# RNN gates of a hybrid block: from three passes for each gate over 128 channels to two passes for both gates of 64 channels

## The chip, the cores and the metric

The kernel runs on 1 core of one Trainium2 chip. The metric is the device time of one execution in microseconds; the time before is the median of three runs, 3054.97 us (3051.18 to 3057.45). A run differs from the next by about 0.1 to 0.2%.

## The reference

Two layers of a transformer-like block work on 512 tokens and on 256 context tokens (in the second layer the context gives only keys, values and the start of the recurrence). Each layer projects the normed input to eight kinds of 1024 columns, and runs three branches side by side: a gated linear recurrence (RG-LRU), differential attention with 8 heads, and a depthwise convolution; a gated merge, a projection and a SwiGLU follow. All of it is float32.

The change is in the recurrence. For each direction `d` and each of 16 blocks of 64 channels there are two small weight matrices of 64x64, `rnn_w_a` and `rnn_w_x`:

```python
r = sigmoid(blockdiag(x, w_a, b_a))          # x: (tokens, 16 blocks, 64) @ (16, 64, 64)
i = sigmoid(blockdiag(x, w_x, b_x))
log_a = -8 * r * softplus(-lam)
a, b = exp(log_a), sqrt(-expm1(2 * log_a)) * (i * x)
h[t] = a[t] * h[t-1] + b[t]                  # d = 0 forward, d = 1 backward; ctx first, its end starts x
y_r = ((h_forward + h_backward) * gelu(gate projection)) @ w_rnn_o
```

## The kernel before

Channels lie on partitions, tokens along the free dimension: 512 of x and 256 of the context, 768 columns in all (`TA`), taken as the two ranges 512 and 256 (`SEG`). A block is 128 channels; a layer has 8. Every large product is a `Job` of the `Stream` (L368, `kstep`): float32 operands are split into a high and a low part of the format fp32r, and high x high, high x low and low x high are added up in PSUM, three passes. The split of the weights is a cast on ScalarE (`whi`, L515) and a subtraction on VectorE (`wlo`, L520), that of activations the same (`split_steps`, L923 and L929).

The order of the instructions of TensorE, ScalarE and VectorE is written out ahead by a planner (`Plan`): each `step` has an engine, an estimated time, what it waits for, a `prio` (the lowest goes first among those that are ready) and slots that it takes (`acq`) and gives back (`rel`): 3 PSUM tiles `sq`, 2 `small`, 11 SBUF tiles `t`, 16 `a`. The engines then follow that order; each is in order. TensorE's steps of prio 9 are the stream of products, whose order is fixed by the list of jobs; all other steps of TensorE go ahead of it when they are ready.

In each layer the list of jobs is, after the convolution's: `rx_job` 0 to 2 and `rg_job` 0 and 1 among fill jobs, eight `c_job`, then for b = 2 to 7 `rx_job(b + 1)`, `rg_job(b)` and `FILL_RNN[l][b]` fill jobs, then the first head's `q_job` and `k_job`, then eight `r_job`. An `r_job` is the product with `w_rnn_o`; it goes through the operand `ar` block by block, so that its last eighth waits for the recurrence of block 7 (`ar[7]`, written at L923 and L929). Nothing of the stream can pass it.

A block's recurrence is this chain: `rx_job` gives the projection; ScalarE takes it out of PSUM (L1071, L1072), VectorE does a 4-tap convolution (L1076 to L1087), `high` and `low` split it into `k.xh` and `k.xl` of 128 partitions (L1098 on ScalarE, L1101 on VectorE). `rg_job`'s start loads the gate weights (four DMAs, L1115) into `gw`, four 128x128 matrices (gate a or x, direction 0 or 1), each with two 64x64 blocks on its diagonal and zeros elsewhere, and splits them (L1120, L1121). `rnn_steps` then has for each direction and gate one `gate` on TensorE (L1163: three passes of 512 and 256 columns) and one `bend` on ScalarE (L1168: tanh of 128x768 out of PSUM). The gates of block b wait for `em` of block b - 1, those of a block share `sq` with the stream. Then follow on ScalarE L1179, L1184, L1187, on VectorE L1190 and L1194, on ScalarE two square roots with a table load before and after them (L1198, L1236), on VectorE L1201, the scans (L1209, L1212), the sum and the product with the gelu (L1216, L1220), and the split into `ar`. Priorities: what empties PSUM for the stream 0, the weights' split 0.5, the gates 1, the bends 2, the rest of the recurrence 3, the sums of the modulation on VectorE (L603) 4.

Of the kernel before, what the change touches and what calls it, by code (L numbers as in the profile page):

```python
# [18 lines left out]
P = 128  # L19
D = 1024  # L20
NB = D // P
S = 512
# [8 lines left out]
# columns of the parameter tile  # L31
# [4 lines left out]
# gate and value blocks after each block of the convolution and before each step of its norm; after each RNN block  # L36
FILL = [[3, 3, 3, 3, 3, 3, 3, 3, 0, 3], [0, 2, 2, 2, 3, 3, 3, 3, 4, 1]]
FILL_RNN = [[0, 0, 0, 1, 0, 0, 2, 0, 0], [0, 0, 0, 0, 1, 1, 1, 0, 4]]
# products of the stream before the second head's scores
# [3 lines left out]
# the blocks of 1024 in the modulation  # L43
SH1, SC1, GA1, SH2, SC2, GA2 = range(6)

class Step:
    """a share of an engine: what it waits for, about how long it takes (us), what it emits, which slots it takes
    and gives back"""
# [6 lines left out]
@functools.lru_cache(None)  # L55
def slots(text):
    """"t2 sq" is two slots of t and one of sq"""
    return tuple((w.rstrip("0123456789"), int(w.lstrip("abcdefghijklmnopqrstuvwxyz") or 1)) for w in text.split())


class Plan:
    """orders what the engines do: a step goes out once its engine is free and what it waits for is there, the
    lowest prio first, by estimates of the times. The tensor engine fills its time from a stream of products."""
# [15 lines left out]
    def chain(self, eng, fns, *deps, prio=2.0):  # L79
        """steps one after the other, each (time, what it emits, slots taken, slots given back)"""  # L80
        for time, f, *sl in fns:
            sl += [""] * (2 - len(sl))
            deps = (self.step(eng, time, f, *deps, prio=prio, acq=sl[0], rel=sl[1]),)
        return deps[0]
# [29 lines left out]
    def run(self, head):  # L114
        """until all is out; head() gives the stream's next step"""
# [32 lines left out]
class Blocks(list):  # L148
    """channel blocks of a product's moving operand, with the steps that make them, for ranges of tokens"""
# [6 lines left out]
class Job:  # L156
    """a block of 128 columns of a product, for (tokens from, how many, place in PSUM); its token ranges at a time"""
# [7 lines left out]
# ranges of tokens where a norm comes between products: from, how many, place in PSUM  # L165
# [14 lines left out]
def kernel(ctx: ExitStack, tc: tile.TileContext, x, c, ctxt, c_ctx, w_mod, b_mod, g_norm1, g_norm2,  # L180
# [24 lines left out]
    def ttr():  # L205
        return tt(F32R)
# [27 lines left out]
    sinT = cp.tile([P, S], F32, tag="sinT", name="sinT")  # L234
    gw = cp.tile([P, 4, P], F32, tag="gw", name="gw")
    gp.memset(gw, 0.0)
# [49 lines left out]
    def param_vec(l, r, ps):  # L286
        r.p = cp.tile([P, NP], F32, tag=f"par{l}", name=f"par{l}")
        vec.tensor_copy(r.p, ps[:, 0:NP])
        # halves for the tanh form of the sigmoid (what stands in front of it and behind it),
        # an eighth for the query  # L290
# [6 lines left out]
    def param_ends(l, r):  # L297
        """the rest of a layer's parameters, as steps"""
# [10 lines left out]
        # c2 = -4 softplus(-lambda); softplus(y) = max(y, 0) + 2 atanh(w / (2 + w)), w = exp(-|y|)  # L309
# [24 lines left out]
        # minus lambda of the differential attention  # L334
# [13 lines left out]
    def mod_scale(r, i):  # L348
        """a norm's gain times 1 + scale"""
# [13 lines left out]
    def kstep(ps, x, hi, lo, k, nk, segs):  # L363
        """adds the k-th 128 channels to a block of the product"""
# [14 lines left out]
    def start():  # L379
# [20 lines left out]
        # the first two blocks of the modulation, 128 columns of both at a time; the first weights between them  # L400
# [42 lines left out]
    # adds up rows 0, 64 and 1, 65 and 32, 96 and 33, 97  # L443
# [15 lines left out]
    class Stream:  # L459
        """the products in order, an eighth of a block a step; weights come two blocks ahead"""  # L460
# [5 lines left out]
        def add(self, items):  # L466
            """blocks one after the other; ("abreast", some) go together, as their operand comes slowly;
            ("ranges", some) by ranges of tokens; ("late", some) wait for the operand's last block together"""
# [24 lines left out]
        def prep(self):  # L493
            """the two parts of the next blocks' weights, where there is a place"""
# [83 lines left out]
    def mod_sums(r, l, b0, b1, nb, ahead_n, *after):  # L578
        """a layer's modulation of channel blocks b0 to b1, its products added up on DVE, nb blocks at a time"""
# [36 lines left out]
        def ends(c, s):  # L616
            box = []

            def rows():
                """three blocks of a vector to a group of 32 rows"""  # L620
# [118 lines left out]
    class Total:  # L739
        """coef times the sum over channels of what comes block by block, on all partitions: four blocks at a time  # L740
        in groups of 32 rows; the last user gives sq back"""
# [39 lines left out]
    class Squares:  # L781
        """the mean over channels of the squares of what comes block by block, for ranges of tokens, tokens on
        partitions: the first blocks' are added up on PE (in groups of 32 rows) or on DVE, the last block's come in
        at the end"""
# [6 lines left out]
        def feed(self, j, src, dep, part=None):  # L791
            """block j, whole or one range of it"""
# [46 lines left out]
        def rstd(self, g=0):  # L839
            """1 / sqrt(the mean + EPS) of a range; tokens on partitions"""  # L840
# [5 lines left out]
            def turn(i):  # L846
                """both sums' columns"""
# [984 lines left out]
```

## Time and profile before

| what | value |
|---|---|
| median of 3 runs | 3054.97 us (3051.18 to 3057.45) |
| profiled execution, first to last instruction | 3049.5 us |
| TensorE busy | 2999.3 us, 98% of the span |
| VectorE busy | 2062.7 us, 68% |
| ScalarE busy | 1345.6 us, 44% |
| mean granted clock of TensorE | 0.994 of full speed |

The page gives the profiled execution's time as its span; the runs' median lies 5.5 us above it, which takes in what is around the first and the last instruction. The share of a busy engine is an average over stages: VectorE and ScalarE are nearly full in some (the recurrence, about 440 to 720 us and 2050 to 2310 us) and half idle in others.

### The profile page before, as it was taken

How to read it: one execution, taken by the hardware profiler on the slowest of the kernel's cores; microseconds unless marked ns; L12 is line 12 of the kernel's file. 1: busy time of each engine (PE TensorE's matmuls, PEld its weight loads, DVE VectorE, ACT ScalarE, POOL GpSimd, SP SyncE). 2: the span in 40 equal slices, each digit the busy share in tenths (PEclk: the TensorE clock that was granted, in tenths of full speed). 3: DMA queues.
4: the chain of work that ended last, by engine and by line, in shares of the span. 5: the costliest groups of instructions: out<-in, count | busy, mean ns of one | idle time of the engine just before them, and what ended most of it. 6: DMA issues, size and time to landing. Idle time of an engine off the chain costs nothing.

```text
span 3049.5 us, 42300 instructions
## 1 busy us (share of the span) xinstructions
PE 2999.3 (98%) x16809; PEld 2535.6 (83%) x16809; DVE 2062.7 (68%) x2934; ACT 1345.6 (44%) x2153; POOL 120.9 (4%) x292
## 2 busy tenths in 40 slices
PE   8999999999999999999999999999999999999999
PEld 6888888888888788888888897888887887888887
DVE  5998887998577754888222269988785777543334
ACT  5222255685377633321111252347784666342223
POOL 0000000000001101000000000000001010000000
PEclk9999999999999999999999999999999999999999
DMA  8322224435321233555222233334235323433332
GB/s 254 98 89 92 85 83 149 154 95 181 106 63 53 80 113 117 170 198 178 63 63 63 63 104 107 119 105 133 80 99 165 89 63 94 139 90 97 97 97 83
DMA packets 451055, 333.34 MB, mean 109 GB/s; under 512 B 24033, under 2 KB 405882, under 8 KB 450857
## 3 DMA queue, kind: packets, MB, share of 16 engines
q1 hardware_dynamic: 442025, 294.71, 31.9%
q0 software_dynamic: 8832, 35.92, 3.3%
q8 instruction: 132, 2.16, 0.3%
q14 instruction: 66, 0.54, 0.1%
HBM read 281.29 MB, written 40.89 MB: 106 GB/s over the span
## 4 chain that ended last, share of the span: by engine, by line
PE 92%; ACT 3%; DVE 2%; SPq 1%; issue 1%; DMA 1%; ACTq 0%; DVEq 0%
PE sq L368 81%; PE sq L1442 4%; PE small L1477 3%; PE small L1468 2%; PE sq L1163 1%; SPq L407 1%; ACT t L1453 1%; PE small L1318 0%; DMA raw<-in_w_ffn_in_dram 0%; PE small L623 0%; DVE wlo L520 0%; PE small L1545 0%; PE small L853 0%; ACT whi L515 0%; ACT t L1168 0%
## 5 line engine op out<-in xcount | busy, mean ns | idle before, releaser
L368 PE MATMUL sq<-u,whi 128*128 128x512 f32 (+1 forms) x6624 | 1597.0, 352 | 7.6 <-ACT t L1301 1.6
L368 PEld LDWEIGHTS sq<-u,whi 128*128 128x128 f32 x6624 | 1069.8, 189 | 185.3 <-issue 8.8
L368 PE MATMUL sq<-u,wlo 128*128 128x512 f32 (+1 forms) x3312 | 968.8, 351 | 1.0 <-DVE wlo L520 1.0
L515 ACT CAST whi<-raw 128x1024 fp32r<-128x1024 f32 (+1 forms) x348 | 360.3, 1036 | 628.9 <-PE sq L368 585.4
L368 PEld LDWEIGHTS sq<-u,wlo 128*128 128x128 f32 x3312 | 540.9, 189 | 85.7 <-DVE wlo L520 1.5
L520 DVE TENSOR_TENSOR wlo<-raw,whi 128x1024 fp32r<-128x1024 f32 (+1 forms) x348 | 420.6, 1209 | 255.5 <-ACT whi L515 252.0
L368 PE MATMUL sq<-a,whi 128*128 128x512 f32 (+1 forms) x2160 | 531.3, 354 | 0.9 <-ACT t L1453 0.5
L995 DVE SCALAR_TENSOR_TENSOR t<-t,par 128x783 f32<-128x783 f32 (+1 forms) x464 | 399.2, 891 | 8.2
L368 PEld LDWEIGHTS sq<-a,whi 128*128 128x128 f32 x2160 | 352.5, 189 | 60.8 <-issue 2.3
L368 PE MATMUL sq<-a,wlo 128*128 128x512 f32 (+1 forms) x1080 | 326.6, 354 | 0.0
L368 PEld LDWEIGHTS sq<-a,wlo 128*128 128x128 f32 x1080 | 179.3, 188 | 28.1
L1575 DVE SCALAR_TENSOR_TENSOR t<-sq,mod,t 128x512 f32<-128x512 f32 (+1 forms) x102 | 62.2, 633 | 200.2 <-PE sq L368 193.7
L603 DVE SCALAR_TENSOR_TENSOR t<-t,sT 128x512 f32<-128x512 f32 (+1 forms) x224 | 185.6, 881 | 7.8 <-DMA t<-in_w_mod_dram 7.7
L1453 ACT ACTIVATE t<-sq,s 128x768 f32<-128x768 f32 (+1 forms) x160 | 130.2, 820 | 42.9 <-DVE s L1446 39.7
L1446 DVE TENSOR_REDUCE s<-sq 128x1 f32<-128x768 f32 (+1 forms) x160 | 128.9, 845 | 29.0 <-PE sq L1442 28.8
L1442 PE MATMUL sq<-t 128*128 128x512 f32 (+3 forms) x576 | 132.1, 402 | 1.3 <-ACT t L1453 1.3
L1634 DVE TENSOR_TENSOR t<-sq,t 128x768 f32<-128x768 f32 (+1 forms) x44 | 36.3, 825 | 141.9 <-PE sq L368 128.9
L1623 ACT ACTIVATE t<-sq 128x768 f32<-128x768 f32 (+1 forms) x44 | 31.0, 705 | 220.3 <-PE sq L368 214.3
L1442 PEld LDWEIGHTS sq<-t 128*128 128x128 f32 (+1 forms) x576 | 72.4, 187 | 54.7 <-issue 38.4
L1301 ACT ACTIVATE t<-sq,par 128x768 f32<-128x768 f32 (+1 forms) x48 | 38.2, 796 | 134.0 <-PE sq L368 133.9
L1257 DVE SCALAR_TENSOR_TENSOR t<-t,sq 128x768 f32<-128x768 f32 (+1 forms) x48 | 39.2, 819 | 75.0 <-PE sq L368 73.2
L1366 ACT CAST t<-t 64x768 fp32r<-64x768 f32 (+3 forms) x96 | 73.2, 762 | 23.0 <-DVE t L1361 16.5
(235 smaller groups left out, 2697.6 us busy)
## 6 DMA issues: line engine op xcount, KB each, us to landing
raw<-in_w_in_dram SPq DMA_DIRECT2D x160, 512.0 KB, 3.8
raw<-in_w_ffn_in_dram SPq DMA_DIRECT2D x88, 512.0 KB, 3.8
t<-in_w_mod_dram SPq DMA_DIRECT2D x64, 384.0 KB, 4.9
t<-in_w_mod_dram SPq DMA_DIRECT2D x64, 256.0 KB, 4.0
raw<-in_w_ffn_out_dram SPq DMA_DIRECT2D x32, 512.0 KB, 3.9
thg<-t POOLq DMA_DIRECT2D x24, 384.0 KB, 2.6
t<-thg SPq DMA_DIRECT2D x24, 384.0 KB, 4.4
raw<-in_w_conv_o_dram SPq DMA_DIRECT2D x16, 512.0 KB, 4.1
```

Source lines behind the costliest of these rows:

```text
L368: pe.matmul(ps[:, at_:at_ + n], a[k], b[:, s0:s0 + n], start=(k == 0 and i == 0), stop=(k == nk - 1 and i == 2))
L515: act.copy(t[:, 0:w], rt[:, q * n:q * n + w])
L520: vec.tensor_sub(o[:, 0:w], rt[:, q * n:q * n + w], t[:, 0:w].bitcast(F32))
L603: vec.scalar_tensor_tensor(a[:, 0:W], tiles[i][:, 0:W], f, a[:, 0:W], op0=ALU.mult, op1=ALU.add)
L995: vec.scalar_tensor_tensor(acc[:, 0:W], zp[:, k:k + W], r.p[:, i:i + 1], acc[:, 0:W], op0=ALU.mult, op1=ALU.add)
L1366: act.copy(x[i][rows, 0:n], t[src, 0:n])
L1442: pe.matmul(sps[m][:, s0:s0 + n], q[2 if i else m][mr, qsl], k[m][mr, s0:s0 + n], start=(i == 0), stop=(i == 1))
L1446: vec.tensor_reduce(mx[:, m:m + 1], sps[m][:, k0:TA], axis=AX.X, op=ALU.max, negate=True)
L1453: act.activation(es[m][:, 0:kw], sps[m][:, k0:TA], AF.Exp, bias=mx[:, m:m + 1], accum_out=sm[:, m:m + 1])
L1468: pe.transpose(tps[:, i:i + P], es[0][:, g0 + i:g0 + i + P], ident)
L1477: pe.matmul(ops[0][:, 0:P], wt[0][:, i * P:(i + 1) * P], vbox[0][:, vb * P:(vb + 1) * P], start=(i == 0), stop=(i == nk - 1))
L1575: vec.scalar_tensor_tensor(hj[:, ss], ps[:, at_:at_ + n], r.mod[:, ga * 8 + j, v:v + 1], hj[:, ss], op0=ALU.mult, op1=ALU.add)
```

## The change

The stationary operand of a gate product now has the a gate and the x gate of the same 64 channels beside each other (64 + 64 columns), and the same weights on both partition halves; the moving operand has the high part of these 64 channels on one half and the low part on the other. One pass gives the high weights times both parts, a second the low weights times both parts. For each direction there are two such products (`e`, the two halves of the block's channels), each followed by two tanh of 64 partitions. For the second half the columns are x gate, a gate, so the output of a gate may lie on the other half than its channels. The casts and subtractions of the split are by halves, each half's after the other's; the weights are loaded twice, once for each partition half; the memset of `gw` goes. The lines that only drop comments are left out.

```diff
-    gp.memset(gw, 0.0)
...
+        half = slice(0, 64), slice(64, P)
...
-                def high():
-                    k.xh, k.xl = ttr(), ttr()
-                    act.copy(k.xh[:, 0:TA], k.xr[:, 0:TA])
-                def low():
-                    vec.tensor_sub(k.xl[:, 0:TA], k.xr[:, 0:TA], k.xh[:, 0:TA].bitcast(F32))
-                e = step(ACT, act_time(TA), high, k.conv, prio=pr, acq="t2")
-                k.parts = step(DVE, vec_time(TA), low, e, prio=pr)
+                def high(e):
+                    if e == 0:
+                        k.x2 = ttr(), ttr()
+                    act.copy(k.x2[e][half[e], 0:TA], k.xr[half[e], 0:TA])
+                def low(e):
+                    vec.tensor_sub(k.x2[e][half[1 - e], 0:TA], k.xr[half[e], 0:TA],
+                                   k.x2[e][half[e], 0:TA].bitcast(F32))
+                k.parts = []
+                for i in range(2):
+                    e = step(ACT, act_time(TA), lambda i=i: high(i), k.conv, *k.parts[-1:], prio=pr,
+                             acq="" if i else "t2")
+                    k.parts.append(step(DVE, vec_time(TA), lambda i=i: low(i), e, prio=pr))
...
-                    for g, wsrc in ((0, rnn_w_a), (2, rnn_w_x)):
+                    for g, wsrc in ((0, rnn_w_a), (1, rnn_w_x)):
                         for e in range(2):
-                            sy.dma_start(gw[64 * e:64 * e + 64, g:g + 2, 64 * e:64 * e + 64],
-                                         wsrc[l, :, 2 * b + e].rearrange("d i o -> i d o"))
+                            c0 = 64 * (g ^ e)
+                            for hr in half:
+                                sy.dma_start(gw[hr, 2 * e:2 * e + 2, c0:c0 + 64],
+                                             wsrc[l, :, 2 * b + e].rearrange("d i o -> i d o"))
...
-            def gate(box, g):
+            def gates_of(box, d, e):
                 box.append(sq())
-                for s0, n in SEG:
-                    for i, (a, x_) in enumerate(((gwh, k.xh), (gwh, k.xl), (gwl, k.xh))):
-                        pe.matmul(box[0][:, s0:s0 + n], a[:, g, :], x_[:, s0:s0 + n], start=(i == 0), stop=(i == 2))
-            def bend(box, to, d, base):
-                to[d] = tt()
-                hb = r.p[:, base + d * 8 + b:base + d * 8 + b + 1]
-                act.activation(to[d][:, A], box[0][:, A], AF.Tanh, bias=hb, scale=0.5)
-            def gated_in(to, d, base, g, *deps):
-                box = []
-                s = step(PE, 0.99, lambda: gate(box, g), k.parts, k.weights, *deps, prio=1 + 0.01 * b, acq="sq t")
-                gates.append(s)
-                return step(ACT, AT, lambda: bend(box, to, d, base), s, prio=2 + 0.01 * b, rel="sq")
+                for i, w in enumerate((gwh, gwl)):
+                    for s0, n in SEG:
+                        pe.matmul(box[0][:, s0:s0 + n], w[:, 2 * e + d, :], k.x2[e][:, s0:s0 + n],
+                                  start=(i == 0), stop=(i == 1))
+            def bend(box, to, d, base, e, x_gate):
+                if e == 0:
+                    to[d] = tt()
+                hb = r.p[half[e], base + d * 8 + b:base + d * 8 + b + 1]
+                act.activation(to[d][half[e], A], box[0][half[e ^ x_gate], A], AF.Tanh, bias=hb, scale=0.5)
+            def gated_in(d, *deps):
+                ends = [(), ()]
+                for e in range(2):
+                    box = []
+                    s = step(PE, 0.7, lambda box=box, e=e: gates_of(box, d, e), k.parts[e], k.weights, *deps,
+                             prio=1 + 0.01 * b, acq="sq" if e else "sq t2")
+                    gates.append(s)
+                    for g, (to, base) in enumerate(((k.th, PBA), (k.ti, PBX))):
+                        s = step(ACT, AT, lambda to=to, base=base, e=e, g=g, box=box: bend(box, to, d, base, e, g),
+                                 s, *ends[g], prio=2 + 0.01 * b, rel="sq" if g else "")
+                        ends[g] = (s,)
+                return ends[0][0], ends[1][0]
...
-                th = gated_in(k.th, d, PBA, d, *before)
-                ti = gated_in(k.ti, d, PBX, 2 + d, *before)
+                th, ti = gated_in(d, *before)
```

The list of jobs, the fill jobs and the slots stay as they are; the planner makes the order anew from the new steps.

## Rows read from the trace of the kernel before

**Rows 1.** The page, busy time of each engine over the span:
```profile
PE 2999.3 (98%) x16809; PEld 2535.6 (83%) x16809; DVE 2062.7 (68%) x2934; ACT 1345.6 (44%) x2153; POOL 120.9 (4%) x292
```

**Rows 2.** The page, chain that ended last, share by engine:
```profile
PE 92%; ACT 3%; DVE 2%; SPq 1%; issue 1%; DMA 1%; ACTq 0%; DVEq 0%
```

**Rows 3.** Timeline of TensorE, one gate and the next's start (start us, us, instruction):
```profile
455.85 0.63 PE L1163 MATMUL sq<-t,gwh 128*128 128x512 f32 x2
456.32 0.40 PE L1163 MATMUL sq<-t,gwl 128*128 128x512 f32 x1
456.55 0.40 PE L1163 MATMUL sq<-t,gwh 128*128 128x256 f32 x2
456.79 0.28 PE L1163 MATMUL sq<-t,gwl 128*128 128x256 f32 x1
456.91 0.63 PE L1163 MATMUL sq<-t,gwh 128*128 128x512 f32 x2
```

**Rows 4.** Timelines of TensorE and VectorE where r_job(0) needs ar[7], both layers:
```profile
720.90 0.62 PE L368 MATMUL sq<-a,whi 128*128 128x512 f32 x2 [0.38 <-DVE a L929]
...
2306.33 0.69 DVE L929 TENSOR_TENSOR a<-t,a 128x512 fp32r<-128x512 f32 x1
...
2306.56 0.85 PE L1468 MATMUL small<-ident,t 128*128 128x128 f32 x6 [3.06 <-DVE t L1459]
...
2307.16 0.70 PE L368 MATMUL sq<-a,whi 128*128 128x512 f32 x2
```

**Rows 5.** Windows from block 2's gates to block 7's roots (PE, PEld, DVE, ACT, POOL busy):
```profile
563.00:706.00 143.00, 141.03 (x815) 121.11 (x814) 141.42 (x189) 119.28 (x144) 2.26 (x15) 1.00 0.35 110
...
2153.00:2292.00 139.00, 138.31 (x694) 116.11 (x693) 116.74 (x142) 124.84 (x156) 3.76 (x15) 1.00 0.31 91
```

**Rows 6.** Windows inside these, each layer's fullest for ScalarE:
```profile
645.00:675.00 30.00, 30.00 (x178) 25.70 (x177) 30.00 (x42) 27.95 (x35) 0.70 (x4) 1.00 0.23 69
...
2238.00:2262.00 24.00, 24.00 (x117) 20.16 (x116) 22.05 (x29) 23.54 (x29) 0.54 (x1) 1.00 0.38 109
```

**Rows 7.** Groups by line on ScalarE, 2153 to 2292 (busy us, mean ns, idle before):
```profile
L1168 ACT ACTIVATE t<-sq,par 128x768 f32<-128x768 f32 x24 | 21.0, 902 | 1.5 <-PE sq L1163 1.5
...
L1098 ACT CAST t<-t 128x768 fp32r<-128x768 f32 x5 | 4.1, 827 | 0.0
```

**Rows 8.** Timelines of ScalarE and VectorE: bends in a row, casts and subtractions of 64 partitions:
```profile
692.70 2.49 ACT L1168 ACTIVATE t<-sq,par 128x768 f32<-128x768 f32 x3
...
718.74 2.54 ACT L1366 CAST t<-t 64x768 fp32r<-64x768 f32 x3
...
725.61 1.94 DVE L1369 TENSOR_TENSOR t<-t 64x768 fp32r<-64x768 f32 x2
```

**Rows 9.** Windows over the c_jobs of each layer:
```profile
493.00:555.00 62.00, 62.00 (x356) 53.23 (x356) 42.31 (x58) 11.45 (x13) 3.96 (x10) 1.00 0.65 213
...
2112.00:2147.00 35.00, 35.00 (x166) 29.32 (x165) 19.33 (x23) 8.88 (x10) 3.59 (x12) 1.00 0.61 191
```

**Rows 10.** Groups by line on VectorE, 563 to 706, and line L1101:
```profile
L603 DVE SCALAR_TENSOR_TENSOR t<-t,sT 128x512 f32<-128x512 f32 x46 | 33.1, 749 | 0.0
...
L1101 DVE TENSOR_TENSOR t<-t 128x768 fp32r<-128x768 f32 x5 | 4.8, 955 | 0.0
```

**Rows 11.** Line L1115, the DMAs of the gate weights (ns min/median/max):
```profile
L1115 SPq DMA_DIRECT2D gw<-in_rnn_w_a_dram x32: 597/607/1907, 430.3 to 2243.8; - x32
```

**Rows 12.** Timeline of VectorE and TensorE before block 7's gates, first layer:
```profile
687.63 0.70 DVE L1121 TENSOR_TENSOR gwl<-gw,gwh 128x512 fp32r<-128x512 f32 x1
...
689.91 0.62 PE L1163 MATMUL sq<-t,gwh 128*128 128x512 f32 x2
```

**Rows 13.** Windows at a fall of TensorE's clock (column after POOL) and at the 3.06 us stall:
```profile
430.00:432.00 2.00, 2.00 (x15) 1.87 (x15) 0.19 (x1) 0.79 (x2) 0.16 (x3) 0.86 0.42 124
432.00:434.00 2.00, 2.00 (x9) 1.71 (x8) 0.00 (x0) 0.76 (x1) 0.00 (x0) 0.50 0.74 200
434.00:436.00 2.00, 2.00 (x15) 1.90 (x15) 0.00 (x0) 0.00 (x0) 0.00 (x0) 0.78 0.02 4
...
2307.00:2311.00 4.00, 4.00 (x27) 3.58 (x26) 2.79 (x5) 1.80 (x3) 0.54 (x1) 1.00 0.02 7
```

## The prediction, made before the changed kernel was run

> **What bounds the kernel now.** I read the busy times first: TensorE is busy 2999 of 3049.5 us, the two other engines that compute 68% and 44% [rows 1]. The chain that ended last says the same, 92% of it is TensorE [rows 2]. So a pass taken off TensorE is worth its whole time, as long as nothing else becomes late. Whether it does is not seen in the averages. Two views show it. The timeline at the point where the product with `w_rnn_o` needs the last block of the recurrence, `ar[7]`, shows that TensorE already waits there in both layers: in the first it stands 0.38 us for L929, which writes `ar[7]`; in the second `ar[7]` is done at 2307.02 (2306.33 + 0.69) and the product goes on at 2307.16, after a stall of 3.06 us [rows 4]. (The stall is put down to an attention step, because six transposes stand ahead of the product in TensorE's queue; it was `ar[7]` too that came only then.) There is no slack at all: if `ar[7]` comes later by some time, all that follows is later by that time, and if TensorE gets to this point earlier while `ar[7]` does not, the gain is lost in a longer stall. The time of the kernel moves with `ar[7]`, once in each layer.
>
> The second view is the windows from block 2's gates to block 7's square roots. ScalarE is busy there 119.3 of 143 us and 124.8 of 139 us, that is 83% and 90%; its average of 44% hides this [rows 1, 5]. In the fullest parts it is at 93% and 98% [rows 6].
>
> **What goes: passes on TensorE.** A gate takes 456.91 - 455.85 = 1.06 us, and one of its three passes, one 512 and one 256 columns wide, 0.35 us [rows 3]. A block has 4 gates of 3 passes before, 4 products of 2 passes after: 4 passes less, 4 x 0.353 = 1.41 us. With 8 blocks in 2 layers it is 22.6 us, 11.3 us for a layer. That is what the change can bring at most: 3054.97 - 22.6 = 3032.4.
>
> **What comes: ScalarE.** A block has 8 bends in place of 4, and 2 casts in place of 1. Does an instruction on 64 partitions cost half? The trace has casts of 64x768: three take 2.54 us, 0.83 for one, and the cast of 128x768 at L1098 takes 0.827 us [rows 7, 8]. So the half costs as much as the whole, and a bend of 64x768 as much as one of 128x768 (it cannot be under half of that, 0.4 us, which I keep as the far end). In a row a bend adds (2.49 - 0.90) / 2 = 0.79 us, by busy time 21.0 / 24 = 0.875 us; a cast 0.74 to 0.82 us [rows 7, 8]. In each of the two windows there are 24 more bends and 5 more casts: 24 x 0.79 + 5 x 0.74 = 22.7 us at least, 24 x 0.875 + 5 x 0.82 = 25.1 us at most. I take 24 us.
>
> Second layer: 124.8 + 24 = 148.8 us of ScalarE work for a stretch that took 139 us. With no gap at all it is longer by 9.8 us; at the best share that the trace has, 98% [rows 6], 151.7 us, longer by 12.7; at the share of before, 90%, 165.7 us, longer by 26.7. ScalarE's gaps of before were mostly waits for TensorE's products, which go when ScalarE is the one behind; I take 98%, +12.7. First layer: 119.3 + 24 = 143.3 for 143 us; without a gap +0.3, at 98% 146.2 us, +3.2, at 93%, that layer's own fullest part [rows 6], 154.1 us, +11.1. I take +3.2. If the planner fitted all of it into gaps, this layer would stay paced by TensorE: its six blocks give back 6 x 1.41 = 8.5 us, less the four bends that block 7 adds after its own gates, 3.2 us, so -5.3; that is the low end.
>
> The stretches begin earlier. Blocks 0 and 1 come before the eight c_jobs, over which ScalarE is busy only 11.5 of 62 and 8.9 of 35 us [rows 9]: what these two blocks add is caught up there, and TensorE comes to block 2 earlier by 2 x 1.41 = 2.8 us in each layer. Sum: first layer 3.2 - 2.8 = +0.4, second 12.7 - 2.8 = +9.9.
>
> **Other edits.** VectorE gets one subtraction more for each block; the 64x768 form takes 0.97 us, as the 128x768 form's 0.955 [rows 8, 10], 15 us in all. In the first layer it is full, 141.4 of 143 us [rows 5], but 33.1 us of that are sums of the modulation, with the last priority [rows 10], which give way and are needed only by the merge much later; cost nothing, and where that cover is missing (second layer, 116.7 of 139 us busy) there are gaps: 0 to 5 us, taken 0. The split by halves delays only the second half: the first half's product waits for one cast and one subtraction as before, the other for two each, 0.8 + 0.97 us later, while the first half's bends run; 0 to 1.8 us a layer, taken 0. Four more DMAs for a block stand in SP's queue at 0.6 us each [rows 11], 2.4 us later for the last and for all weights queued behind them. The weights of the stream come two blocks ahead, so they have cover; the gate weights of block 7 in the first layer do not: they are split by 688.3 us and its gates start at 689.9 [rows 12]. 0 to 2.4 us there, taken 0 since the bends then wait for ScalarE anyway. The memset of `gw`: nothing. Two `t` slots taken together in place of one after the other: 0, at worst a gate held back for one step of about 1 us.
>
> **The clock.** TensorE would come to `r_job(0)` 11.3 us earlier and find `ar[7]` 0.4 and 9.9 us later, so the stalls grow to some 12 and 24 us, at one place or several. The only fall of the clock in this stage has no stall before it: after 24 one-column products the granted clock is 0.86, 0.50 (1.2 GHz) and 0.78 in three windows of 2 us, a loss of (0.14 + 0.50 + 0.22) x 2 = 1.7 us; after the 3.06 us stall the clock stayed at 1.00, 2.4 GHz [rows 13]. Stalls four or more times as long have no row. I count one fall of 1.7 us (0 to two of them, 3.4). The Trainium skill (TensorE: Matmul & The Clock Gate, section "Why this matters for your kernels") warns of idle gaps between bursts of products, after which the clock goes back to half speed until the engine has again been kept busy. By that rule both stalls would cost a fall and the term would be 3.4 us; by the row at 2307 none, and 0. No run here has yet shown which.
>
> **Sum.** +0.4 + 9.9 + 1.7 = +12.0 us on the profiled execution's 3049.5, that is 3061.5 for the span. The runs' median is 5.5 us above that span; the difference is kept, so 3054.97 + 12.0 = 3067.
>
> **Rivals.** (1) *TensorE keeps the pace, the passes are gained.* The work on ScalarE that stands before `ar[7]` is not all of the recurrence; if enough of it (the evacuations of fill jobs, the casts for the first head's q and k, the gelu) goes after it, `ar[7]` comes earlier with TensorE's stream and the time is 3032.4, or half that gain with one layer, about 3043. For it: ScalarE has 23.7 us of gaps in the first layer's stretch, as much as is added [rows 5]. Against it: those other steps stand before the recurrence by priority, and the 148.8 us of the second layer do not fit into 139 us less the 8.5 that TensorE saves. (2) *A draw.* First layer paced by TensorE, -5.3 - 2.8 = -8.1 us; second without a gap, +9.8 - 2.8 = +7.0; together -1.1, or 3054. The point from which it decides is whether ScalarE is filled over 98% in the second layer and stays under TensorE's pace in the first. (3) *Gaps stay.* The recurrence is a chain over ScalarE and VectorE with only two blocks in flight, so ScalarE can't be filled: at 93% and 90%, 11.1 + 26.7 - 5.6 + 3.4 = +35.6, 3091. For it: these are the shares of before; against it: what ended the gaps then. (4) *Half instructions cost half*: then ScalarE gets nothing more, and it is case 1; the casts speak against it [rows 8].
>
> **Chances.** My forecast (ScalarE sets the time of `ar[7]`, 3057 to 3082) 0.52; case 3 beyond it 0.12; the draw, 3047 to 3061, 0.18; cases 1 and 4 0.18. A measurement of this kernel tells 0.2%, 6 us, from no change. Of the forecast's chance some 0.06 lies within 6 us above, and the draw's lies mostly within it: faster 0.20, within 0.2% 0.22, slower 0.58. The range for 8 in 10 leaves out the full gain of case 1 and the far end of case 3: 3041 to 3085; the forecast alone has 3057 to 3082.
>
> **What would show it.** Right: the products of L1163 fall from 384 to 256 and by some 22 us of spacing; L1168 has 128 instructions of 64x768 at about 0.9 us each, so 50 us more on ScalarE; ScalarE's share from block 2's gates to block 7's roots is over 95% in the second layer; TensorE waits over 15 us in all before `r_job(0)`'s last eighth or at products held back by `sq`, and TensorE's busy time is about 22 us less though the span is longer. Wrong: `ar[7]` of the second layer earlier than 2307 us, or bends of 64 partitions that take half; or a stall of this kind that is there, but as long as before.

## The result: slower, by more than five times the forecast

The changed kernel takes 3120.31 us (median of 4 runs, 3118.06 to 3125.07) against 3053.07 (3050.07 to 3057.45): ratio 1.0224, interval 1.0209 to 1.0238, or +67.2 us. The forecast was +12, its range ended at 3085. The sign and the mechanism hold (ScalarE sets the time of `ar[7]`), the size doesn't.

The page after, busy times and (the second line) the chain that ended last:

```profile
PE 3010.4 (97%) x16681; PEld 2534.4 (81%) x16681; DVE 2084.8 (67%) x2950; ACT 1427.9 (46%) x2238; POOL 120.3 (4%) x291
...
PE 86%; ACT 7%; DVE 3%; issue 1%; SPq 1%; DMA 1%; ACTq 0%; DVEq 0%
```

Against [rows 1, 2]: TensorE has 128 products less, as the change says, and yet is busy 11.1 us longer; ScalarE has 82.3 us more, and 7% of the chain in place of 3%. The span of the profiled execution is 3116.3 us. Over TensorE its +66.8 us are -22.6 for the passes (a block's four products take 4 x 0.70 us after, the first from 453.86 to 454.56; its four gates took 4 x 1.06), +55.7 idle (50.2 before, 105.9 after), and, as the rest, +33.7 by which it was busy without more work. Most of that is a lower clock: TensorE was busy for 27.5 us at a granted clock of 0.50 before and for 75.0 us after, of which half, 13.8 and 37.5 us, is lost, so 23.7 us more. For the other 10 us no row here has a cause.

Groups by line after, on ScalarE (busy us, mean ns, idle before):

```profile
L1180 ACT ACTIVATE t<-sq,par 64x768 f32<-64x768 f32 x128 | 113.5, 895 | 6.1 <-PE sq L1173 3.8
L1100 ACT CAST t<-t 64x768 fp32r<-64x768 f32 x32 | 26.5, 829 | 0.4
...
L1180 ACT ACT_TABLE_LOAD x6 | 7.7, 1283 | 0.1
```

A bend of 64 partitions lasts 895 ns, one of 128 lasted 902 [rows 7]: half the work at the whole price. 64 bends more and 16 casts more are there, and table loads that belong to a bend, of which the kernel before had one: in the new order a bend of the next block falls between the square roots and the reload of the table that follows them.

Where the time came in is seen at `ar[7]`. TensorE's timeline after, at the point of [rows 4] in the first layer:

```profile
735.94 0.51 PE L368 MATMUL sq<-a,wlo 128*128 128x512 f32 x2
748.78 2.00 PE L368 MATMUL sq<-a,whi 128*128 128x512 f32 x4 [12.32 <-ACT a L923]
```

VectorE's timeline after, the writes of `ar[7]` in both layers:

```profile
748.76 0.96 DVE L929 TENSOR_TENSOR a<-t,a 128x768 fp32r<-128x768 f32 x1 [0.90 <-ACT a L923]
...
2371.38 0.69 DVE L929 TENSOR_TENSOR a<-t,a 128x512 fp32r<-128x512 f32 x1 [0.74 <-ACT a L923]
```

The stall of 0.38 us became one of 12.32 us, and `ar[7]` is done at 749.7 and 2372.1 us; before it was 720.8 and 2307.0. The last c_job's sum on VectorE marks the start of each stretch, the part from there to `ar[7]`. Before:

```profile
547.15 0.95 DVE L1257 SCALAR_TENSOR_TENSOR t<-t,sq 128x768 f32<-128x768 f32 x1
...
2139.26 0.69 DVE L1257 SCALAR_TENSOR_TENSOR t<-t,sq 128x512 f32<-128x512 f32 x1 [2.15 <-PE sq L368]
```

After:

```profile
548.27 0.95 DVE L1276 SCALAR_TENSOR_TENSOR t<-t,sq 128x768 f32<-128x768 f32 x1 [0.67 <-PE sq L368]
...
2173.21 0.69 DVE L1276 SCALAR_TENSOR_TENSOR t<-t,sq 128x512 f32<-128x512 f32 x1 [2.15 <-PE sq L368]
```

So the span grew by 1.1 us up to the first stretch, 27.8 in it, 5.1 from there through the second layer's first two blocks and c_jobs, 31.1 in the second stretch, and 1.7 after it: 66.8 in all.

The two stretches as windows, in the kernel before (PE, PEld, DVE, ACT, POOL busy, TensorE's granted clock, DMA share, GB/s):

```profile
560.00:721.00 161.00, 158.65 (x917) 136.31 (x915) 159.42 (x217) 126.66 (x153) 2.26 (x15) 1.00 0.39 121
2147.00:2307.00 160.00, 156.25 (x783) 130.41 (x783) 134.96 (x166) 138.29 (x178) 4.30 (x16) 1.00 0.32 94
```

The same of the changed kernel:

```profile
560.00:749.00 189.00, 162.24 (x887) 135.58 (x886) 174.92 (x234) 160.41 (x187) 2.26 (x15) 0.93 0.37 111
2180.00:2370.00 190.00, 161.88 (x744) 130.39 (x742) 140.61 (x170) 168.91 (x210) 4.29 (x16) 0.92 0.28 83
```

This is the main reading. ScalarE's work grew by 33.8 and 30.6 us, the stretches by 28 and 30, and the time in which ScalarE stood idle hardly moved: 161 - 126.66 = 34.3 us became 28.6, and 21.7 became 21.1. Its share is 85% and 89% after, not the 98% that the forecast was built on. Its work was added to the time nearly one for one. VectorE, which was full in the first layer before (159.4 of 161 us), stands idle there for 14 us after, so it isn't what makes that stretch longer.

What TensorE waited for after, whole span (us in total, times, longest):

```profile
PE sq L1173 <- ACT t L1180: 19.0, 11, 5.7
PE sq L368 <- ACT t L1180: 15.8, 10, 2.8
PE sq L368 <- ACT a L923: 12.3, 1, 12.3
PE small L1487 <- DVE t L1478: 5.0, 3, 4.2
PE sq L368 <- ACT t L1140: 4.1, 1, 4.1
```

Much of the idle time isn't one stall at `r_job(0)`: 34.8 us are products, of the gates and of other jobs, that wait for a bend to give a PSUM tile back.

### The profile page after: what moved, and what is told of

Read it like the earlier page. It is cut to its first block, busy times and chain, and to the rows that moved or that the text cites. A ratio compares the mean times of both kernels' runs of the same rounds, so it can differ in the third digit from the quotient of the medians.

```text
span 3116.3 us, 42301 instructions
## 1 busy us (share of the span) xinstructions
PE 3010.4 (97%) x16681; PEld 2534.4 (81%) x16681; DVE 2084.8 (67%) x2950; ACT 1427.9 (46%) x2238; POOL 120.3 (4%) x291
## 4 chain that ended last, share of the span: by engine, by line
PE 86%; ACT 7%; DVE 3%; issue 1%; SPq 1%; DMA 1%; ACTq 0%; DVEq 0%
PE sq L368 76%; PE sq L1461 3%; PE small L1496 3%; ACT t L1180 2%; PE small L1487 2%; SPq L407 1%; ACT whi L515 1%; ACT t L1472 1%; DVE wlo L520 0%; DMA raw<-in_w_ffn_in_dram 0%; PE sq L1173 0%; PE small L1337 0%; ACT t L1199 0%; ACT t L1204 0%; PE small L623 0%
## 5 line engine op out<-in xcount | busy, mean ns | idle before, releaser
L1180 ACT ACTIVATE t<-sq,par 64x768 f32<-64x768 f32 x128 | 113.5, 895 | 6.1 <-PE sq L1173 3.8
```

Source lines behind the costliest of these rows:

```text
L1180: act.activation(to[d][half[e], A], box[0][half[e ^ x_gate], A], AF.Tanh, bias=hb, scale=0.5)
```

## Experiments

Each ratio is against runs of the kernel before on the same chip (medians 3051 to 3054). "Done" is when the last L929 of a layer ends, the time of `ar[7]`.

| kernel | us | ratio, interval | against before | done, first layer | done, second |
|---|---|---|---|---|---|
| before | 3053.1 | 1 | 0 | 720.8 | 2307.0 |
| changed | 3120.3 | 1.0224, 1.0209 to 1.0238 | +67.2 | 749.7 | 2372.1 |
| e1, whole bends | 3045.0 | 0.9976, 0.9966 to 0.9985 | -6.6 | 712.3 | 2301.0 |
| e2, before + half bends | 3101.4 | 1.0164, 1.0149 to 1.0179 | +49.8 | 743.6 | 2355.8 |
| e3, before + half split | 3061.3 | 1.0034, 1.0021 to 1.0047 | +9.8 | 722.0 | 2312.1 |
| e4, planner told times | 3129.9 | 1.0257, 1.0242 to 1.0272 | +78.4 | 756.1 | 2379.1 |
| e5, less gelu | 3104.7 | 1.0173, 1.0159 to 1.0187 | +53.6 | 743.6 | 2350.5 |
| e6, square on VectorE | 3109.3 | 1.0190, 1.0176 to 1.0204 | +58.2 | 753.4 | 2364.2 |
| e7, before + eight DMAs | 3055.4 | 1.0015, 1.0006 to 1.0025 | +4.3 | 721.0 | 2309.8 |
| e8, changed in blocks 0, 1 | 3068.8 | 1.0057, 1.0045 to 1.0070 | +17.7 | 729.5 | 2320.5 |
| e9, before + copies | 3095.2 | 1.0136, 1.0121 to 1.0152 | +41.4 | 744.2 | 2350.5 |
| e10, products in the stall | 3116.4 | 1.0213, 1.0196 to 1.0230 | +62.7 | 752.0 | 2374.2 |
| e11, changed, four DMAs | 3121.1 | 1.0228, 1.0211 to 1.0245 | +68.6 | 749.6 | 2369.8 |

The second layer's `ar[7]` moves with the time in every row, to within about 10 us; it carries the kernel's time, as the prediction had it.

**e1, the passes without the half bends.** One bend of 128 partitions follows each product in place of two:

```diff
-                    for g, (to, base) in enumerate(((k.th, PBA), (k.ti, PBX))):
-                        s = step(ACT, AT, ... bend(box, to, d, base, e, g), ...)
+                act.activation(to[d][:, A], box[0][:, A], AF.Tanh, bias=hb, scale=0.5)
```

> The changed kernel, but each two-pass product is read by one tanh of 128x768 (a product e = 0 into th, e = 1 into ti) in place of two of 64x768. What is left out: each half's own gate and bias, so th and ti hold mixed halves. Passes, split, DMAs as changed; ScalarE has 4 bends for a block, as before. Theory A (the added ScalarE work in the bends makes ar[7] late): the 64 bends taken away cost 64 x 0.92 = 59 us of ScalarE time; the gain of the passes comes out nearly whole, 3035 to 3050 us, L1173 idles fall from 19 to under 5 us. Rival B (what delays is not the bends but the split by halves, the eight DMAs or the form of the product): stays above 3090. Rival C (PSUM is held by two readers): as A, this run does not part it from A.

-6.6 us. Its page:

```profile
PE 2986.1 (98%) x16681; PEld 2518.6 (83%) x16681; DVE 2079.0 (68%) x2950; ACT 1361.8 (45%) x2172; POOL 121.9 (4%) x291
```

All of the change is in it but the 64 added bends and the second reader of each tile. Those (with two table loads more, 66.1 us of ScalarE) then cost 67.2 + 6.6 = 73.8 us of time.

**e2, the half bends without the passes.** The kernel before, each bend as two halves of 64 partitions:

```diff
+                hs = slice(64 * e, 64 * e + 64)
-                act.activation(to[d][:, A], box[0][:, A], AF.Tanh, bias=hb, scale=0.5)
+                act.activation(to[d][hs, A], box[0][hs, A], AF.Tanh, bias=hb, scale=0.5)
```

> The kernel before, three passes, with each bend of 128x768 done as two of 64x768; nothing left out. Theory A: ScalarE gets the same 57 to 60 us as in the changed kernel, so ar[7] is late by nearly as much in both layers although no pass is saved: 3100 to 3135 us. Rival B: the bends alone cost little, 3053 to 3070. If the passes saved do count beside the bends (ScalarE not the pace everywhere), this run lies 10 to 22 us above the changed kernel, 3130 to 3142.

+49.8 us with 62.6 us more on ScalarE, on a kernel whose TensorE work is unchanged. Its TensorE waits:

```profile
PE sq L1163 <- ACT t L1170: 11.4, 7, 3.6
PE sq L368 <- ACT a L923: 9.7, 1, 9.7
PE sq L368 <- ACT t L1170: 5.8, 5, 2.2
```

The same three waits as in the changed kernel. Three quarters of the loss need no new layout of the product. The run lies 17 us under the changed kernel, not 10 to 22 above it, so the passes saved don't show beside the half bends.

**e3, the split by halves alone**, as in the change, on the kernel before:

```diff
-                    act.copy(k.xh[:, 0:TA], k.xr[:, 0:TA])
+                    act.copy(k.xh[half[e], 0:TA], k.xr[half[e], 0:TA])
```

> The kernel before with the high and low part of x made by halves (2 casts and 2 subtractions of 64x768, one after the other), all else as before; nothing left out. Theory A: 16 x 0.85 = 14 us more ScalarE work, a quarter of that of the bends, so 3055 to 3070 us. Rival B (the serial split is what delays the gates): 3085 to 3120.

+9.8 us with 18.7 us more on ScalarE. A gate of this kernel reads both halves, so it waits for the second one; in the changed kernel only every second product does.

**e4, the planner's times set to what the halves take** (0.92, 0.86 and 0.97 us):

```diff
-                        s = step(ACT, AT, ...bend...)
+                        s = step(ACT, 0.92, ...bend...)
```

> The changed kernel, only the planner's times of the new steps set to what the trace shows: a bend of 64x768 0.92 us (it had 0.777), a cast 0.86, a subtraction 0.97. Nothing left out. Rival D (the engines' order is wrong because the planner thinks the bends are shorter; TensorE then stands at gates whose PSUM tile is not free yet, 19 us at L1173 and 16 us at products behind them): those idles halve and the time falls to 3075 to 3100. Theory A alone: ScalarE's work is the same, so within 10 us of 3120.

Slower still, by some 11 us over the changed kernel. It has 9 table loads more (76 in place of 67), but up to the second `ar[7]`, which comes 7.0 us later, it has 3 less (59 in place of 62). Truer estimates in the planner don't bring the loss back.

**e5, ScalarE work off the gates' chain taken away**: the square and the tanh of the gelu.

```diff
-                    act.activation(k.gx[:, 0:T], rg[:, 0:T], AF.Square, bias=pb(O_RG, b), scale=1.0)
...
-                    act.activation(k.gx[:, 0:T], k.gx[:, 0:T], AF.Tanh, scale=GELU * 0.044715)
```

> The changed kernel without two ScalarE instructions of each block that stand beside the recurrence's chain: the square and the tanh of the gelu (L1140, L1147). Left out: the gelu's tanh, so the gate is a polynomial; VectorE's instructions are the same. It takes about 8 x 2 x 0.8 + 8 x 2 x 0.6 = 22 us off ScalarE, nothing off the chain from a block's gates to the next block's. Theory A1 (ScalarE's capacity in the recurrence sets ar[7], 0.8 us of time for 1 us of ScalarE, as e2's 49.8 us for 62.6 us): faster by 15 to 20 us, 3100 to 3105. Theory A2 (the chain's length sets it: products, bends, tanh, exp, square, next gates): within 5 us of 3120.

13.6 us better than the changed kernel, though ScalarE's busy time over the whole span fell only from 1427.9 to 1422.1: the new order has 11 table loads more (78), 14 us. The added ones lie behind the second `ar[7]` (17 there in place of 5); up to it ScalarE is busy 1093.9 us in place of 1115.5. So 21.5 us less of work gave back 13.6 us of time, nearer to theory A1 than to A2: work beside the chain counts too. The run also gives the PSUM tile of the gelu's product back one instruction earlier, which wasn't tried apart.

**e6, the square of the decay moved to VectorE**, on the chain itself:

```diff
-                act.activation(k.th[d][:, A], k.al[d][:, A], AF.Square)
+                vec.tensor_mul(k.th[d][:, A], k.al[d][:, A], k.al[d][:, A])
```

> The changed kernel with the square of the decay (L1207, 32 of 128x768) on VectorE in place of ScalarE; nothing left out. 32 x 0.8 = 26 us off ScalarE, on the chain, where an instruction of 0.95 us with a change of engine takes the place of one of 0.85 us. Theory A1: faster by 15 to 25 us, 3095 to 3105, as VectorE has room in the second layer and low work to push away in the first. Theory A2: the chain is a little longer, so 3118 to 3130.

9 us better for 23.9 us less on ScalarE, between the two theories. The second layer's `ar[7]` comes 7.9 us earlier, the first's 3.7 later. VectorE was full in the first layer before the change [rows 5] and is busy 186.6 of the 193 us from 560 to 753 here. TensorE's long wait in the first layer is now put down to the modulation's sums, which the forecast had called cover:

```profile
PE small L623 <- DVE t L603: 16.0, 2, 15.2
```

It would have waited for `ar[7]` without them: behind the products of these sums it still stands 0.49 us for L923 before it goes on with `r_job(0)` at 752.41.

**e7, eight DMAs for a block's gate weights** in the kernel before, of the same bytes:

```diff
-                            sy.dma_start(gw[64 * e:64 * e + 64, g:g + 2, 64 * e:64 * e + 64],
-                                         wsrc[l, :, 2 * b + e].rearrange("d i o -> i d o"))
+                            for d in range(2):
+                                sy.dma_start(gw[64 * e:64 * e + 64, g + d, 64 * e:64 * e + 64], wsrc[l, d, 2 * b + e])
```

> The kernel before with the gate weights loaded by eight DMAs for a block (one for each direction) in place of four, the same bytes; nothing left out. All theories: 2.4 us more in SP's queue for a block, and only block 7 of the first layer has gate weights without cover: 3051 to 3057. If the part of e1 that the split (e3, +9.8 us) does not explain, -6.6 + 22.6 - 9.8 = 6.2 us, were the DMAs, 3057 to 3060.

+4.3 us (the interval begins at +2). The changed kernel's eight move twice these bytes, which this run leaves out. **e11** is its counterpart, the changed kernel with four:

```diff
-                            for hr in half:
+                            for hr in half[:1]:
```

> The changed kernel with 4 of a block's 8 DMAs of gate weights: the second copy of the weights, on the partitions of the low part (of the high part for the other half of the channels), is left out and stays zero, so the products miss that part. In the changed kernel ScalarE stands 15.4 us in five waits for gate weights (before: 7.5 us in two); the cast of these weights stands in its queue ahead of bends. With eight DMAs in the kernel before it was 16.9 us in six waits and 4.3 us of time. Theory A (ScalarE and its waits set the time between block 2 and ar[7], so that each us of a wait of its own counts): the waits fall to some 7.5 us and the time by 4 to 8 us, 3112 to 3116. Rival B (with half bends ScalarE is behind anyway, the weights' late landing is covered by it): under 2 us, 3118 to 3122.

The waits fell, as this line of ScalarE's waits shows (15.4 us in five before the edit), and the time didn't:

```profile
ACT gwh L1130 <- DMA gw<-in_rnn_w_x_dram: 5.9, 1, 5.9
```

Its runs spread from 3114.3 to 3126.8, so a gain of a few us could hide in them. As far as they tell, rival B is the nearer one: the late weights are covered by ScalarE's own delay in the changed kernel.

**e8, blocks 0 and 1 of each layer as changed, the others as before**:

```diff
+                if b in NEW:    # (0, 1)
                     th, ti = gated_in(d, *before)
+                else:
+                    th = gated_in1(k.th, d, PBA, d, *before)
```

> Blocks 0 and 1 of each layer as in the changed kernel, blocks 2 to 7 as before (with a memset of gw ahead of block 2's weights); nothing left out. Behind blocks 0 and 1 come the eight c_jobs, over which ScalarE is busy 11.5 of 62 and 8.9 of 35 us. Theory A (ScalarE's added work costs where it is full): what is added is caught up there and 4 x 1.41 = 5.6 us of passes are gained: 3044 to 3051 beside 3051.5 of before. Rival: the added work costs as much there as elsewhere, a quarter of 67 us: 3063 to 3072.

+17.7 us: a quarter of the blocks costs a quarter of the loss. The last c_job's sum of each layer in this run:

```profile
549.91 0.95 DVE L1316 SCALAR_TENSOR_TENSOR t<-t,sq 128x768 f32<-128x768 f32 x1 [0.66 <-PE sq L369]
...
2152.54 0.69 DVE L1316 SCALAR_TENSOR_TENSOR t<-t,sq 128x512 f32<-128x512 f32 x1 [2.15 <-PE sq L369]
```

The first is 2.8 us later than before, the first `ar[7]` 8.7, the second sum 13.3, the second `ar[7]` 13.5. So blocks 0 and 1, which stand before the c_jobs, are not caught up over them: 2.8 and 4.6 us are lost there, where a gain was forecast. The other 10 us come later, 5.9 of them in the first layer's stretch, whose blocks have the form of before; the run doesn't show why. Two windows at the gates of blocks 0 and 1 in the first layer, of the kernel before:

```profile
450.00:460.00 10.00, 10.00 (x60) 8.73 (x58) 8.30 (x11) 8.66 (x13) 0.00 (x0) 1.00 0.18 52
460.00:470.00 10.00, 8.60 (x49) 7.20 (x49) 7.96 (x10) 9.97 (x14) 0.00 (x0) 1.00 0.25 67
```

Of the changed kernel:

```profile
450.00:460.00 10.00, 7.48 (x42) 5.98 (x40) 8.70 (x11) 8.72 (x12) 0.00 (x0) 0.97 0.18 52
460.00:470.00 10.00, 7.97 (x25) 6.46 (x26) 6.17 (x8) 9.80 (x12) 0.00 (x0) 0.52 0.44 120
```

Of e8:

```profile
450.00:460.00 10.00, 8.86 (x52) 7.55 (x51) 8.37 (x11) 8.91 (x13) 0.00 (x0) 1.00 0.19 53
460.00:470.00 10.00, 6.59 (x23) 5.01 (x24) 7.71 (x10) 9.79 (x12) 0.00 (x0) 0.66 0.30 77
```

ScalarE is full at this place before the change already (9.97 of 10), which the averages over the later c_jobs [rows 9] don't show. In the second window TensorE gets 25 and 23 instructions through in place of 49, at a clock of 0.52 and 0.66.

**e9, ScalarE's time on the chain without the PSUM tiles**: the kernel before, and after each whole bend a copy of 64x768 in place.

```diff
-                return step(ACT, AT, lambda: bend(box, to, d, base), s, ..., rel="sq")
+                s = step(ACT, AT, lambda: bend(box, to, d, base), s, ..., rel="sq")
+                return step(ACT, AT, lambda: act.copy(to[d][0:64, A], to[d][0:64, A]), s, ...)
```

> The kernel before, with a copy of 64x768 in place on ScalarE after each bend, on the path to the logarithm, the decay and the inputs; the PSUM tile goes back after the one bend, as before; the copies change nothing that is computed. As many instructions more on ScalarE as with half bends in the kernel before (64), which took 62.6 us more of busy time and 50 us more of time. Theory A (the price of half bends is ScalarE's time on the chain of the recurrence): 64 copies at 0.74 to 0.92 are 47 to 59 us of busy time, and at 0.8 us of time for each the kernel gets 38 to 47 us longer, 3089 to 3098. Theory B (the price is that a PSUM tile goes back only after two readers, so that TensorE's products wait for one of three tiles): no product waits longer for its tile here, so less than half of 50 us, under 3076, and TensorE's stalls are not at its gates but at the place where ar[7] is read.

+41.4 us, as theory A had it. TensorE's waits:

```profile
PE sq L368 <- ACT a L923: 20.1, 3, 15.1
PE sq L368 <- ACT t L1131: 4.8, 3, 3.6
...
PE sq L1163 <- ACT t L1168: 1.8, 1, 1.8
```

The waits at the gates are all but gone, and `ar[7]` is late all the same, in the first layer with one stall of 15.1 us. Where TensorE stands is a symptom; ScalarE's added time ahead of `ar[7]` is the cause. The copies are 51.6 us of busy time, 0.80 us of time for each; 16 table loads more (78 to the 62 of before) belong to this run too, but 12 of them lie behind the second `ar[7]`. The windows from the start to the second `ar[7]`, of the kernel before, e2, e9 and the changed kernel, count ScalarE's work up to there (the fourth busy time):

```profile
0.00:2307.02 2307.02, 2270.03 (x13064) 1931.28 (x13065) 1672.85 (x2352) 1032.42 (x1568) 94.76 (x254) 0.99 0.36 112
0.00:2355.78 2355.78, 2288.69 (x13062) 1940.48 (x13063) 1674.06 (x2352) 1094.85 (x1634) 95.22 (x254) 0.99 0.35 110
0.00:2350.47 2350.47, 2286.09 (x13079) 1942.54 (x13079) 1675.46 (x2353) 1086.40 (x1640) 95.27 (x254) 0.99 0.36 110
0.00:2372.07 2372.07, 2279.08 (x12948) 1928.53 (x12949) 1694.85 (x2368) 1115.46 (x1655) 94.17 (x253) 0.98 0.36 110
```

That is 62.4 us more in e2 for +49.8 of time, and 54.0 in e9 for +41.4: 0.80 and 0.77 us for each. So e2's 8.4 us more of time go with 8.5 us more of work, and little is left for the PSUM tiles. What e9 doesn't part is the chain's length from ScalarE's load: its copies add to both.

**e10, 40 products in the 12.32 us stall**, to hold the clock:

```diff
+            if k == 7 and getattr(j, "warm", False):
+                ps = small()
+                for _ in range(40):
+                    pe.matmul(ps, j.xs[0][0][:, 0:P], j.xs[0][0][:, 0:512], start=True, stop=True)
```

> The changed kernel, with 40 products of 512 columns, whose sum nobody reads, ahead of the last eighth of the first block of the product with w_rnn_o in the first layer, where TensorE stood idle for 12.32 us; at full clock they take some 8.5 us (40 x 0.213). Theory A (the stall costs more than its length, since TensorE starts again at half its clock): with the products in the stall the windows after it are at 1.00 in place of 0.50 to 0.78 between 748 and 754 us, and the product goes on as far behind ar[7] as before, so 2 us are won (3.2 us at 0.50 and 2 us at 0.78), 3118, if ScalarE and VectorE don't set the pace there. Rival B (the clock falls for what came ahead of the stall, not for the stall): the windows stay at 0.50 to 0.78 and the 40 products take up to 17 us, longer than the stall, so some 5 us are lost, 3125.

3116.44 us; its interval overlaps that of the changed kernel, so in time nothing is shown. The windows do show something. The changed kernel, from the stall on (the clock is the column after POOL):

```profile
745.00:748.00 3.00, 0.00 (x0) 0.00 (x0) 2.79 (x3) 0.11 (x1) 0.00 (x0) 0.50 0.00 0
748.00:750.00 2.00, 1.22 (x3) 0.74 (x4) 0.96 (x1) 0.72 (x1) 0.00 (x0) 0.50 0.00 0
750.00:752.00 2.00, 2.00 (x7) 1.72 (x8) 0.54 (x1) 1.04 (x1) 0.00 (x0) 0.50 0.00 0
752.00:754.00 2.00, 2.00 (x11) 1.69 (x10) 1.97 (x3) 0.00 (x0) 0.30 (x1) 0.78 0.00 0
```

The run with the 40 products:

```profile
744.00:746.00 2.00, 2.00 (x10) 1.68 (x9) 1.97 (x4) 0.00 (x0) 0.00 (x0) 1.00 0.00 0
746.00:748.00 2.00, 1.32 (x6) 0.75 (x4) 2.00 (x2) 0.00 (x0) 0.00 (x0) 1.00 0.00 0
748.00:750.00 2.00, 0.00 (x0) 0.00 (x0) 1.93 (x3) 0.00 (x0) 0.00 (x0) 1.00 0.00 0
750.00:752.00 2.00, 0.61 (x2) 0.30 (x2) 1.07 (x2) 0.83 (x1) 0.00 (x0) 0.94 0.00 0
752.00:754.00 2.00, 1.97 (x6) 1.69 (x7) 0.29 (x1) 0.93 (x1) 0.00 (x0) 0.50 0.00 0
```

The 40 products took 9.24 us. With them the clock stays at 1.00 to 750, where it had been 0.50 from 745 on. But `ar[7]` came 2.3 us later in this run, a stall of 3.71 us was left, and the clock fell after that one. Rival B falls in its first part: the stall makes the fall. What it is worth in time stays open.

## Why the prediction was wrong

**The step that failed: "I take 98%".** The forecast let the new ScalarE work flow into ScalarE's gaps, because they "were mostly waits for TensorE's products, which go when ScalarE is the one behind". They don't go: 34.3 us of gaps became 28.6, 21.7 became 21.1. A reading that fits is that the recurrence is a chain over the engines with few blocks in flight, so that a longer link makes the chain longer and what stands beside it waits with it. It is not shown apart from ScalarE's load: e9's copies add to both, and e5, which takes work away beside the chain, won 13.6 us too. Rival 3 said that gaps stay, took the shares of before and got 3091; it had a chance of 0.12 and was nearest, 29 us short. The 98% was read from a window of 24 us [rows 6]; it is the best of one short stretch, and no layer came near it. In the terms of the sum, +3.2 for the first stretch became +27.8, +12.7 for the second +31.1, and -2.8 for blocks 0 and 1 of each layer +1.1 and +5.1; what the clock costs lies within these.

**The price of the work.** 24 us a layer was 28.7 us in both stretches; another 5.1 and 1.9 us is work that fell into them from outside as they grew. Bends 22.0 us (24 more, 0.9 each), casts 4.1, table loads 2.6, which the forecast didn't have. The spacing "0.79" came from whole bends. Halves mostly stand wider; ScalarE's timeline after:

```profile
459.25 2.74 ACT L1180 ACTIVATE t<-sq,par 64x768 f32<-64x768 f32 x3
...
632.38 5.49 ACT L1180 ACTIVATE t<-sq,par 64x768 f32<-64x768 f32 x6
...
693.71 3.39 ACT L1180 ACTIVATE t<-sq,par 64x768 f32<-64x768 f32 x4
```

(5.49 - 0.90) / 5 = 0.92 us from one to the next in the first two rows, (3.39 - 0.90) / 3 = 0.83 in the last. At 0.92 a block's bends take 8 x 0.92 - 4 x 0.79 = 4.2 us more, not 3.2; by busy time, 22.0 us for six blocks, it is 3.7. A row shown ahead of the prediction said so: three casts of 64 partitions in 2.54 us [rows 8] are 0.86 apart, wider than one is long, where whole bends overlap.

**"Caught up over the c_jobs".** Wrong: the forecast had counted blocks 0 and 1 as a gain of 2.8 us a layer. Up to the end of the c_jobs they cost 1.1 and 5.1 us in the changed kernel, 2.8 and 4.6 in e8. ScalarE was already full at their gates, so that their products waited there; the c_jobs' own rows don't show that.

**The passes.** -22.6 us is right as work: the change removes 128 products. As time it is gained only while ScalarE's work stays as it was: e1 shows -6.6, and if the parts add up, 9.8 (e3) and 4.3 (e7) of the rest lie in the split and the DMAs, -8.5 by that sum. Once the half bends are in, nothing is left of it: e2, e3 and e7, which all keep the three passes, add up to 49.8 + 9.8 + 4.3 = 63.9 us, and the change with two passes loses 67.2. That TensorE's gain is lost in a longer stall is what the prediction had said.

**Taken as nothing.** The split was worth 9.8 us by itself (0 to 1.8 a layer was the bound; it is ScalarE work like the bends). The DMAs were 4.3 us by themselves and, by e11, little or nothing beside the bends. VectorE's one subtraction more was covered as assumed, as far as its idle time in the stretches tells; in e6, with VectorE nearly full in the first layer, `ar[7]` came 3.7 us later there.

**The clock.** "One fall of 1.7 us" against 23.7 us more that TensorE lost while busy at a clock of 0.50; the granted clock of the whole run fell from 0.994 to 0.983, and is 0.93 and 0.92 in the two stretches. The fall at the 12.32 us stall is as foreseen, two windows at 0.50 and one at 0.78 after TensorE goes on. What was missed is that shorter waits at the gates do it too. TensorE's timeline after, ahead of the clock's 0.52 at 460 to 470 us:

```profile
457.61 0.62 PE L1173 MATMUL sq<-t,gwh 128*128 128x512 f32 x2 [1.14 <-ACT t L1073]
...
460.20 1.01 PE L1173 MATMUL sq<-t,gwh 128*128 128x512 f32 x2 [1.58 <-ACT t L1180]
```

The rule of the Trainium skill (TensorE: Matmul & The Clock Gate, section "Why this matters for your kernels") is that the clock goes back after idle gaps between bursts. The falls at the stalls of 12.32 us and, in e10, of 3.71 us agree with it, unlike the row at 2307 us that I had set against it. The gaps of 1.14 and 1.58 us are shorter than those it warns of; there the trace decides. How much of the 23.7 us reaches the end isn't settled: where ScalarE sets the pace, a slower TensorE only fills a stall, but a slow gate also delays its bend.

**Right.** Half instructions cost as much as whole ones, TensorE waits more than 15 us at `r_job(0)` or for `sq`, `ar[7]` is later than 2307, the time moves with it. **Not as said:** ScalarE over 95%, and TensorE's busy time 22 us less.

## What to carry to other kernels

When two engines pass a chain back and forth, don't fill the gaps of the second one with added work: price added work at about its full busy time until a trace shows the gaps shrink. Here each us on ScalarE cost or gave back 0.8 us of time in e2 and e9, 0.5 in e3, 0.6 in e5, 0.4 in e6, and 1.1 for the half bends where the passes were gone (e1 against the changed kernel). A change that saves the busiest engine 22.6 us by giving its neighbour twice as many instructions has to be priced by the neighbour's instruction count, not by the data in each, since half the partitions cost the whole time. Split the change into its parts before judging it: all but the half bends gave -6.6, the parts alone +49.8, +9.8 and +4.3, which no view of the changed kernel shows.

## What the runs showed of the hardware

- A tanh of 64x768 out of PSUM on ScalarE lasts 0.895 us, one of 128x768 0.902. Whole bends in a row start 0.79 us apart. Half bends mostly start 0.92 us apart (the row at 632.38), but some stand closer (0.83 on average in the row at 693.71), so the 64 partitions don't prevent the overlap by themselves; what does was not found.
- The granted clock was 0.50 at the end of an idle time of 12.32 us and for some 4 us after it. After 3.71 us of idle time in e10 it fell as well, to 0.50 between 752 and 754 us, where after the 3.06 us stall of the kernel before it had stayed at 1.00 [rows 13]. In the changed kernel it fell after two gaps of 1.14 and 1.58 us too, to 0.52 on average from 460 to 470 us.
